# Half sums made one per step, a third wide pair of gate blocks, and a way down that starts later and runs behind every column tile, in a four-layer fp32 trunk on one Trainium2 core

## The chip, the cores and the metric

The kernel runs on 1 core of one Trainium2 chip. The metric is the device time of one execution in microseconds. The kernel before takes 1391.58 us (median of three runs, 1390.59 to 1392.77). The profile quoted below is of one further execution.

## The reference, cut to what matters

A trunk of two layers for 512 tokens of width 1024, all in float32. Each layer is a token mixer (attention in layer 0, a gated linear recurrence in layer 1) and then a gated feed-forward with a short causal convolution. Each of the four parts is normed before and after and added to the residual stream. The feed-forward is the part that most of the change is in:

```python
def conv_ffn(x, w_up, conv_w, conv_b, w_down):          # x 512x1024, w_up 1024x6144, w_down 3072x1024
    u = causal_dwconv(x @ w_up, conv_w, conv_b)          # three taps
    g, v = u[..., :D_FF], u[..., D_FF:]                  # gate and value, 3072 columns each
    return (jax.nn.gelu(g, approximate=True) * v) @ w_down
```

The attention's projection is `x @ w_qkv`, 1024 by 9216.

## The kernel before, in words

**Numbers in two parts.** Every float32 matrix product is made of three matmuls: each operand is split into a high part (written as fp32r by ACT, line 253 for weights) and the rest (by DVE, line 265), and `PASSES` multiplies high by high, high by low and low by high. A unit of weights is one such pair of tiles, `whi` and `wlo`. Eight units exist (`W_UNITS`). After each piece of work on PE the kernel calls `tick()`, which lets side work run (`run_sides`) and calls `pump`, which splits one or two further units in the order of a plan. So a unit is split up to eight units ahead of its use, and ACT and DVE take their work strictly in the order in which it was written.

**Where weights come from.** A plain piece of weights is loaded by SP (line 340) into one of two `raw` buffers of 1 MB; the next load into a buffer stands in SP's queue until both units in it have been split. A piece that is the sum of two pieces of the matrix is built in the one tile `sum`: a first DMA writes one addend (line 309, on SP in the later parts of the kernel), and a second DMA on POOL adds the other (line 311, accumulating). A sum that needs both is a chain: the tile's last reader, the first DMA, the accumulating DMA, then the split on ACT and DVE.

**The feed-forward's way up.** There are 24 gate column blocks and 24 value column blocks of 128, taken in six pairs of steps (`PAIRS`). A plain column tile (`feat_tiles`, `feat`, matmuls on line 436) is 24 matmuls of 128 columns by 512 tokens into a PSUM tile `ps`. In a pair marked True ("wide") the four gate blocks are made together by `sevenths`: seven products of half size in place of eight, each 24 matmuls of 128 columns by 256 tokens (line 870) into `W`, `X` or `Z`, with weights that are sums of weight pieces and right-hand sides `T` that are sums of token halves. The four value blocks of such a pair stay plain tiles. So a plain pair has eight plain tiles; a wide pair has four plain tiles and seven products.

**The token sums.** `token_sums.make` forms the `T`s once per feed-forward, in four names (3, 2, 4, 1), each in two halves `h`: one to three additions on DVE (line 630, tile `run`), a cast on ACT (line 610) at the start of the next step, and the low part on DVE (line 587 or 585) behind the next half's additions. A side task steps through it: one half, then as many ticks as `TOKEN_PACE` says. The attention uses the same helper with a pace of 1.

**The way down.** 3072 rows of `w_down` are done in two units of 1024 rows by seven products each (`down_unit`, `product`, 24 matmuls of 128x512 on line 650, banks `W`, `X`, `vq`) and then 1024 plain rows (`rows_proj`, tiles `acc`). The two units' fourteen products are laid between the column tiles of the later pairs: from step `DOWN_FROM` on, the column tiles are counted f = 0, 1, 2, ..., and a product follows the tiles listed in `DOWN_AT`. I call the products P1 to P14; P1 to P7 are the first unit. The weights of P1, P3, P5 (and P8, P10, P12) are plain pieces (`value`); those of P2, P4, P6, P7 and P9, P11, P13, P14 are in the `sum` tile. P4 and P6 (P11 and P13) only add to what stands in the tile, on POOL alone; P2, P7, P9 and P14 need the first DMA and the accumulating one. The left operands of the products (`A`) are made from the gated columns in `operands`: sums on DVE (line 940), the cast on ACT (944 or 947), the low part on DVE (587, 585 or 953). Results are copied by ACT (line 591, tile `c`), combined on DVE (line 665) and, for the first unit, written to HBM (`down`, line 978, SP).

Of the kernel before, what the change touches and what calls it, by code (L numbers as in the profile page):

```python
# [40 lines left out]
CP_PAD = 8  # L41
WARM = 6

PAIRS = [([0, 1], False), ([2, 3], True), ([4, 5], True), ([6, 7], False), ([8, 9], False), ([10, 11], False)]
DOWN_FROM = 6
DOWN_UNITS = 2
DOWN_AT = (3, 5, 6, 7, 8, 9, 12, 13, 15, 16, 17, 18, 19, 22)
WIDE_STEPS = (1, 3, 1, 2)
TOKEN_PACE = (1, 1, 1, 1, 2, 2, 2, 1)

SHORT_ORDER = [
    ([0, 1], [0, 1, 2]), ([0], [3]), ([2, 3], [0]), ([1], [3]), ([2, 3], [1]), ([2], [2, 3]), ([3], [2, 3]),
# [43 lines left out]
def kernel(  # L96
# [41 lines left out]
    def nm(s):  # L138
        uid[0] += 1
        return f"{s}{uid[0]}"  # L140

    def gen(dt=F32, s="g"):
        return gp.tile([P, 512], dt, tag="g", name=nm(s))
# [45 lines left out]
    raws, units, late, since = {}, {}, [], {}  # L189
# [177 lines left out]
    def side(steps, delay=1, late=False, first=False):  # L367
        sides.insert(0 if first else len(sides), [delay, steps, late])

    def tick():  # L370
        state["tick"] += 1
        run_sides(False)
        if not state["hold"]:
            pump(1 if state["live"] >= W_UNITS - 2 else 2)
        if state["rows"]:
            low_parts()
            loads()
        run_sides(True)
# [201 lines left out]
    def corner(hT, i, j):  # L580
        return lambda a: hT[a][:, 4 * i : 4 * i + 4, j * 256 : (j + 1) * 256]

    def low(lo, whole, hi, flip=False):
        if flip:
            nc.vector.scalar_tensor_tensor(lo, whole, -1.0, hi.bitcast(F32), op0=ALU.mult, op1=ALU.subtract)
        else:
            nc.vector.tensor_tensor(lo, whole, hi.bitcast(F32), op=ALU.subtract)
# [6 lines left out]
    def token_sums(hT):  # L594

        made = {}
        terms_of = {
            3: [((1, 1), 1), ((0, 1), -1)],
            2: [((0, 0), 1)],
            4: [((1, 0), -1)],  # L600
            1: [((0, 0), 1), ((0, 1), -1)],
        }

        def make(pace):
            pace = iter(pace)
            prior, begun = None, []

            def high():
                for hi, lo, a, flip in begun:
                    nc.scalar.activation(hi, a, AF.Copy, scale=-1.0 if flip else 1.0)  # L610

            def lows():
                for hi, lo, a, flip in begun:
                    low(lo, a, hi, flip)
                begun.clear()

            for name in (3, 2, 4, 1):
                hi, lo = (htp.tile([P, 4, 256], F32R, tag="x", name=nm("T"), bufs=8) for _ in range(2))
                made[name] = hi, lo
                parts = [(corner(hT, *ij)(x).bitcast(F32), sg) for ij, sg in terms_of[name] for x in range(2)]  # L620
                if name in (3, 1):
                    first = parts.pop(0)[0]
                    prior = [first[:, 2 * h : 2 * h + 2] for h in range(2)]
                r = [gen(s="run").rearrange("p (k c) -> p k c", k=2) for _ in range(2)]
                for h in range(2):
                    k = slice(2 * h, 2 * h + 2)
                    a = prior[h]
                    high()
                    for b, sg in parts:
                        nc.vector.tensor_tensor(r[h], a, b[:, k], op=ALU.add if sg > 0 else ALU.subtract)  # L630
                        a = r[h]
                    lows()
                    begun.append((hi[:, k], lo[:, k], a, name == 2))
                    yield next(pace)
                prior = r
            high()
            lows()

        return (lambda name: lambda a: made[name][a]), make
# [194 lines left out]
    def ffn(layer, hT, post, pre, spill):  # L834
# [25 lines left out]
        total_of, make = token_sums(hT)  # L860
# [120 lines left out]
        def down_units():  # L981

            ops = (op for n in range(DOWN_UNITS) for op in operands(8 * n))
            for _ in range(2):
                begin_operand(ops)
                end_operand()
                yield
            for n in range(DOWN_UNITS):
                yield from down_unit(n, ops)
            write()  # L990
# [72 lines left out]
        units, at_feat = down_units(), [0]  # L1063
        for js, wide in PAIRS:
            n = state["next"]
            steps = sevenths(js[0], n) if wide else None
            at = iter(WIDE_STEPS if wide else ())

            def between():
                for _ in range(next(at, 0)):  # L1070
                    next(steps, None)
                    tick()
                if j >= DOWN_FROM:
                    f = at_feat[0]
                    if f < 2 or f in DOWN_AT:
                        next(units)
                    if f in DOWN_AT:
                        if f == DOWN_AT[-2]:
                            state["slots"] += 2
                        tick()  # L1080
                    at_feat[0] += 1

            for j in js:
                if j == 11:
                    prep(5)
                if j == 1:
                    side(make(TOKEN_PACE))

                def sink(b, ps):
                    gated(2 if wide else b, ps, 2 * j + b % 2)  # L1090

                feat_tiles(1 if wide else 2, hT, sink, j == 0, between, (n + 3 + 3 * (j - js[0])) if wide else None)
            if wide:
                state["next"] += 9
# [6 lines left out]
    def attention(hT, post, pre, spill):  # L1101
# [411 lines left out]
        total_of, make = token_sums(hT)  # L1513
# [9 lines left out]
        def to_local(p, s, tiles):  # L1523
            local_v[p].extend(tiles)
# [12 lines left out]
        for hp in range(4):  # L1537
            q, k = [], []
            if hp == 0:
                c, o = first_values()  # L1540
                to_local(0, 0, o)
                steps = value_all(c)
                side(make([1] * 8), late=True)
                side(build, late=True)
            v = local_v[hp // 2]
            sink = qk_sink(q, k, False, True, not hp)
            for j in range(2):
                feat_tiles(1, hT, lambda m, ps: sink(2 * j + m, ps), not (hp or j), paired=False)
                step("l", hp, j)
            for hh in range(2):  # L1550
                side(local(2 * hp + hh, hh, q, k, v), 1 + hh)
# [211 lines left out]
    for layer in range(2):  # L1763
# [10 lines left out]
        downs, feats = down_quarters(layer, ends), 0  # L1774
        for js, wide in PAIRS:
            if not wide:
                for j in js:
                    for c0 in (0, D_FF):
                        n = w_cols(w_up, c0 + j * 256, own=False)
                        for m in range(2):  # L1780
                            split_next(n, m)
                            if j >= DOWN_FROM:
                                if feats in DOWN_AT:
                                    next(downs)
                                feats += 1
                continue
            a, b = (j * 256 for j in js)
# [96 lines left out]
```

## Time and profile before

| What | Number |
|---|---|
| Three runs | 1392.77, 1391.58, 1390.59 us; median 1391.58 |
| The profiled execution | 1388.06 us |
| Its span | 1386.3 us |
| Granted TensorE clock, mean | 0.994 |
| PE busy | 98% of the span |
| DVE busy | 74% |
| ACT busy | 50% |

The span is the time from the first instruction to the last in the profiled execution; the execution's own time is 1.8 us more, and the median of the three runs is 3.5 us above the profiled execution. PE matmuls overlap, and the durations that the profile gives them are longer than the distance from one start to the next; I read the cost of a matmul from starts. In the rows, the idle time of an engine before an instruction, and what ended it, stand in brackets. The first feed-forward (layer 0) is the one with times from about 520 to 860 us, the second from about 1040 to 1386 us.

### The profile page before, as it was taken

Reading aid. Unit: us, or ns where it says so; the run is one execution under the profiler, and the core shown is the slowest. Engines: PE = TensorE matmul, PEld = TensorE weight load, DVE = VectorE, ACT = ScalarE, POOL = GpSimd, SP = SyncE. Lnnn points to the kernel's source line nnn. Section 1 sums busy time; section 2 is a strip of 40 time slices with the busy share of each in tenths; the row PEclk is TensorE's granted clock in tenths of the full one; section 3 lists DMA queues with packets and bytes.
Section 4 is the critical chain, followed back from the end, with each engine's and each line's share of the span. In section 5 each row is a group of like instructions: output and inputs, shape, how many; then the busy total and the mean of one; then the engine's idle time right before and its main releaser. Section 6 shows DMA issues by size and latency. Waiting matters only on the chain.

```text
span 1386.3 us, 18707 instructions
## 1 busy us (share of the span) xinstructions
PE 1356.7 (98%) x7109; PEld 1201.8 (87%) x7109; DVE 1027.0 (74%) x1790; ACT 692.7 (50%) x1169; POOL 111.7 (8%) x126
## 2 busy tenths in 40 slices
PE   8989999999999999999999999999999999999997
PEld 6878888888888889898888889888899898888886
DVE  7777574636767689777958769878979777968765
ACT  5434442414355554455645545579664455645542
POOL 2111012011000001000000110000001000000110
PEclk9999999999999999999999999999999999999999
DMA  8878879596648355555668793233154555768671
GB/s 258 226 206 231 227 190 260 192 211 193 224 153 304 100 176 122 149 168 122 199 171 196 209 259 122 92 122 122 62 162 113 152 162 130 208 180 196 197 187 61
DMA packets 184236, 243.10 MB, mean 175 GB/s; under 512 B 16632, under 2 KB 135936, under 8 KB 184146
## 3 DMA queue, kind: packets, MB, share of 16 engines
q1 hardware_dynamic: 151456, 184.82, 40.5%
q0 software_dynamic: 32688, 57.09, 21.4%
q8 instruction: 56, 0.92, 0.3%
q14 instruction: 34, 0.28, 0.1%
q10 hardware_dynamic: 2, 0.00, 0.0%
HBM read 218.23 MB, written 28.36 MB: 178 GB/s over the span
## 4 chain that ended last, share of the span: by engine, by line
PE 47%; DVE 17%; ACT 5%; issue 2%; DMA 1%; DVEq 0%; ACTq 0%; SPq 0%
PE ps L436 24%; PE acc L436 8%; PE X L650 4%; DVE wlo L265 4%; PE vq L650 3%; PE W L650 3%; DVE u L843 2%; PE X L870 2%; DVE run L630 2%; DVE xb L1603 1%; PE Z L870 1%; DVE x L551 1%; PE W L870 1%; ACT whi L253 1%; DMA sum<-in_ffn_w_up_dram 1%
## 5 line engine op out<-in xcount | busy, mean ns | idle before, releaser
L436 PE MATMUL ps<-hT,whi 128*128 128x512 f32 (+1 forms) x2528 | 698.3, 362 | 0.8 <-DVE hT L499 0.6
L436 PEld LDWEIGHTS ps<-hT,whi 128*128 128x128 f32 x2528 | 459.5, 190 | 57.8 <-issue 1.3
L436 PE MATMUL ps<-hT,wlo 128*128 128x512 f32 (+1 forms) x1264 | 456.6, 361 | 4.7 <-DVE wlo L265 4.7
L265 DVE TENSOR_TENSOR wlo<-raw,whi 128x1024 fp32r<-128x1024 f32 x233 | 279.8, 1217 | 36.6 <-ACT whi L253 36.5
L253 ACT ACTIVATE whi<-raw 128x1024 fp32r<-128x1024 f32 x233 | 239.4, 1051 | 120.2 <-DMA raw<-in_attn_w_qkv_dram 87.1
L436 PEld LDWEIGHTS ps<-hT,wlo 128*128 128x128 f32 x1264 | 240.0, 190 | 33.5 <-DVE wlo L265 5.5
L843 DVE SCALAR_TENSOR_TENSOR u<-ps,cols,u 128x511 f32<-128x511 f32 (+1 forms) x160 | 119.6, 747 | 72.0 <-ACT u L839 69.0
L253 ACT ACTIVATE whi<-sum 128x1024 fp32r<-128x1024 f32 x68 | 70.8, 1053 | 124.0 <-DMA sum<-in_attn_w_qkv_dram 70.8
L265 DVE TENSOR_TENSOR wlo<-sum,whi 128x1024 fp32r<-128x1024 f32 x68 | 82.0, 1217 | 43.1 <-ACT whi L253 43.1
L436 PE MATMUL acc<-whi,ahi 128*128 128x512 f32 x256 | 98.2, 383 | 0.0
L436 PE MATMUL acc<-wlo,ahi 128*128 128x512 f32 x256 | 97.1, 379 | 0.3 <-DVE wlo L265 0.3
L436 PE MATMUL acc<-whi,alo 128*128 128x512 f32 x256 | 97.1, 379 | 0.0
L839 ACT ACTIVATE u<-ps,cols 128x512 f32<-128x512 f32 x80 | 61.6, 771 | 39.4 <-PE ps L436 39.2
L853 ACT ACTIVATE u<-u 128x512 f32<-128x512 f32 x48 | 30.3, 631 | 96.5 <-DVE u L843 96.4
L650 PE MATMUL vq<-whi,T 128*128 128x512 f32 x192 | 59.7, 382 | 0.0
L650 PE MATMUL X<-whi,A 128*128 128x512 f32 x192 | 59.0, 379 | 0.0
L436 PEld LDWEIGHTS acc<-whi,alo 128*128 128x128 f32 x256 | 48.4, 189 | 7.3 <-DVE alo L185 0.4
L436 PEld LDWEIGHTS acc<-wlo,ahi 128*128 128x128 f32 x256 | 48.4, 189 | 7.1 <-DVE wlo L265 0.7
L436 PEld LDWEIGHTS acc<-whi,ahi 128*128 128x128 f32 x256 | 48.4, 189 | 6.6 <-ACT ahi L184 0.2
L311 POOL DMA_DIRECT2D sum<-in_ffn_w_down_dram x16 | 20.6, 1289 | 363.4 <-DMA sum<-in_ffn_w_down_dram 124.0
L855 DVE TENSOR_TENSOR u<-u,u 128x512 f32<-128x512 f32 x48 | 33.2, 692 | 13.5 <-ACT u L853 12.4
L650 PEld LDWEIGHTS X<-whi,A 128*128 128x128 f32 x192 | 36.3, 189 | 5.2
(252 smaller groups left out, 1974.9 us busy)
## 6 DMA issues: line engine op xcount, KB each, us to landing
raw<-in_ffn_w_up_dram SPq DMA_DIRECT2D x44, 1024.0 KB
raw<-in_attn_w_qkv_dram SPq DMA_DIRECT2D x25, 1024.0 KB
raw<-in_ffn_w_down_dram SPq DMA_DIRECT2D x16, 1024.0 KB
sum<-in_ffn_w_down_dram POOLq DMA_DIRECT2D x16, 1024.0 KB, 8.8
sum<-in_attn_w_qkv_dram POOLq DMA_DIRECT2D x24, 512.0 KB, 7.8
raw<-in_attn_w_qkv_dram SPq DMA_DIRECT2D x16, 512.0 KB
sum<-in_ffn_w_down_dram SPq DMA_DIRECT2D x8, 1024.0 KB
raw<-in_lru_w_in_dram SPq DMA_DIRECT2D x8, 1024.0 KB
```

The lines of the kernel that those rows point to most:

```text
L253: nc.scalar.activation(hi, raw, AF.Copy)
L265: nc.vector.tensor_tensor(lo, raw, hi.bitcast(F32), op=ALU.subtract)
L311: nc.gpsimd.dma_start(dst, src, accum_op=ALU.add)
L436: mm(dst, l[a], r[b], start=start and n == 0, stop=stop and n == 2)
L551: nc.vector.scalar_tensor_tensor(xh[i], u[i], y, xh[i], op0=ALU.mult, op1=ALU.add)
L630: nc.vector.tensor_tensor(r[h], a, b[:, k], op=ALU.add if sg > 0 else ALU.subtract)
L650: mm(banks[u], act(a)[:, 2 * j + k, u * P : (u + 1) * P], woven(W[b][:, k, :]), start=first and (j, k, n) == (0, 0, 0), stop=(j, k, n) == ...
L839: nc.scalar.activation(u, ps, AF.Identity, scale=cc[:, j : j + 1], bias=cc[:, 48 + j : 49 + j])
L843: nc.vector.scalar_tensor_tensor(u[:, d:], ps[:, : S - d], wc, u[:, d:], op0=ALU.mult, op1=ALU.add)
L853: nc.scalar.activation(u, u, AF.Gelu_apprx_tanh)
L855: nc.vector.tensor_tensor(gv[k], gv[k], u, op=ALU.mult)
L870: mm(bank[:, n * 256 : (n + 1) * 256], W[a][:, k, n * P : (n + 1) * P], woven(act(b)[:, k, :]), start=first and (n, k, p) == (0, 0, 0), st ...
```

## The change

Five edits:

1. The fourth pair (steps 6 and 7) becomes wide: its four gate blocks go through `sevenths`.
2. The way down starts two steps later (`DOWN_FROM` 8 and not 6), so its column tiles are counted over 16 tiles, f = 0 to 15.
3. `DOWN_AT` puts one product behind every column tile from f = 2 to f = 15. Before, the fourteen products stood over f = 3 to 22, with one or two tiles without a product at places: two ahead of P7, one ahead of P9, two ahead of P14.
4. `TOKEN_PACE` is 1 throughout, so the halves of the token sums follow each other at every tick.
5. `make` takes a second argument. In the feed-forward (`behind` true) the cast stands as before at the start of the next step. In the attention (`behind` false) the cast on ACT is written at once behind the half's additions.

```diff
-PAIRS = [([0, 1], False), ([2, 3], True), ([4, 5], True), ([6, 7], False), ([8, 9], False), ([10, 11], False)]
-DOWN_FROM = 6
+PAIRS = [([0, 1], False), ([2, 3], True), ([4, 5], True), ([6, 7], True), ([8, 9], False), ([10, 11], False)]
+DOWN_FROM = 8
 DOWN_UNITS = 2
-DOWN_AT = (3, 5, 6, 7, 8, 9, 12, 13, 15, 16, 17, 18, 19, 22)
+DOWN_AT = (2, 3, 4, 5, 6, 7, 8, 9, 10, 11, 12, 13, 14, 15)
 WIDE_STEPS = (1, 3, 1, 2)
-TOKEN_PACE = (1, 1, 1, 1, 2, 2, 2, 1)
+TOKEN_PACE = (1, 1, 1, 1, 1, 1, 1, 1)
...
-        def make(pace):
+        def make(pace, behind):
             pace = iter(pace)
-            prior, begun = None, []
+            prior, whole, begun = None, [], []
 
             def high():
-                for hi, lo, a, flip in begun:
+                for hi, lo, a, flip in whole:
                     nc.scalar.activation(hi, a, AF.Copy, scale=-1.0 if flip else 1.0)
+                begun.extend(whole)
+                whole.clear()
...
                     lows()
-                    begun.append((hi[:, k], lo[:, k], a, name == 2))
+                    whole.append((hi[:, k], lo[:, k], a, name == 2))
+                    if not behind:
+                        high()
                     yield next(pace)
...
-                    side(make(TOKEN_PACE))
+                    side(make(TOKEN_PACE, True))
...
-                side(make([1] * 8), late=True)
+                side(make([1] * 8, False), late=True)
```

Lines of the changed kernel behind the edits stand two to four lower (630 becomes 632, 650 becomes 654, 870 becomes 874).

The program of the changed kernel shows what moved at three places. The first is ACT in the attention, at the second and third token sums. `T` is a token sum's high part, `run` its additions, `whi` a weight's high part, and `sum` and `raw` the weights' sources; first the kernel before.

```order
L253 ACTIVATE whi105_493<-raw86_374 128x1024
L610 ACTIVATE T94_412<-run97_415 128x512
L1177 ACTIVATE qk111_529<-ps88_377 128x512
L253 ACTIVATE whi112_531<-sum55_231 128x1024
L610 ACTIVATE T107_497<-run109_499 128x512
L253 ACTIVATE whi122_581<-sum55_231 128x1024
L610 ACTIVATE T107_497<-run110_500 128x512
```

The same place in the changed kernel:

```order
L253 ACTIVATE whi105_494<-raw86_374 128x1024
L610 ACTIVATE T107_498<-run109_500 128x512
L1181 ACTIVATE qk111_530<-ps88_377 128x512
L253 ACTIVATE whi112_532<-sum55_231 128x1024
L610 ACTIVATE T107_498<-run110_501 128x512
L253 ACTIVATE whi122_582<-sum55_231 128x1024
```

The cast of `T107`'s first half stood behind the split of a `sum` and now stands ahead of it; every later cast moved up by a step in the same way. DVE's order in the attention is the same in both.

The second place is DVE in the first feed-forward, at the last token sum (name 1: `run992`, `run993` and `T991` before; `run982`, `run983` and `T981` after). `T968` is the sum ahead of it, `w` an output of a wide pair. The kernel before:

```order
L587 TENSOR_TENSOR T968_4975<-run970_4977,T967_4974 128x512
L265 TENSOR_TENSOR wlo985_5084<-sum920_4603,whi984_5083 128x1024
L265 TENSOR_TENSOR wlo995_5128<-raw982_5055,whi994_5127 128x1024
L219 TENSOR_TENSOR sum920_4603<-sum920_4603 128x1024
L843 SCALAR_TENSOR_TENSOR u1000_5188<-ps999_5163,cols364_1815,u1000_5188 128x511
L843 SCALAR_TENSOR_TENSOR u1000_5188<-ps999_5163,cols364_1815,u1000_5188 128x510
L630 TENSOR_TENSOR run993_5121<-hT0780_3932,hT1781_3933 128x512
L630 TENSOR_TENSOR run993_5121<-run993_5121,hT0780_3932 128x512
L630 TENSOR_TENSOR run993_5121<-run993_5121,hT1781_3933 128x512
L587 TENSOR_TENSOR T991_5119<-run992_5120,T990_5118 128x512
L265 TENSOR_TENSOR wlo998_5161<-sum920_4603,whi997_5160 128x1024
```

The changed kernel, from the same low part of `T968`:

```order
L587 TENSOR_TENSOR T968_4975<-run970_4977,T967_4974 128x512
L265 TENSOR_TENSOR wlo977_5019<-raw947_4817,whi976_5018 128x1024
L632 TENSOR_TENSOR run983_5054<-hT0780_3932,hT1781_3933 128x512
L632 TENSOR_TENSOR run983_5054<-run983_5054,hT0780_3932 128x512
L632 TENSOR_TENSOR run983_5054<-run983_5054,hT1781_3933 128x512
L587 TENSOR_TENSOR T981_5052<-run982_5053,T980_5051 128x512
L265 TENSOR_TENSOR wlo985_5061<-raw960_4900,whi984_5060 128x1024
L893 TENSOR_TENSOR w992_5128<-c987_5090,Z991_5103 128x256
L893 TENSOR_TENSOR w993_5129<-c987_5090,Z991_5103 128x256
L587 TENSOR_TENSOR T981_5052<-run983_5054,T980_5051 128x512
L265 TENSOR_TENSOR wlo989_5098<-sum920_4603,whi988_5097 128x1024
```

The last token sum is complete ahead of the split that reads `sum920`, and ahead of the addition on line 219; before, it came behind both.

The third place is SP's queue in the first feed-forward's way down, from the results of P4 on. `down` is a write of results, `raw` a load of plain weights, and `sum` the first DMA of a sum. The kernel before:

```order
L978 DMA down909_4495<-c1101_5939 128x512
L309 DMA sum1062_5659<-in_ffn_w_down_dram 128x4x512
L340 DMA raw1159_6314<-in_ffn_w_down_dram 128x4x512
L978 DMA down909_4495<-c1145_6224 128x512
L978 DMA down909_4495<-c1146_6226 128x512
L340 DMA raw1177_6405<-in_ffn_w_up_dram 128x8x256
L309 DMA sum1062_5659<-in_ffn_w_down_dram 128x4x512
L340 DMA raw1186_6477<-in_ffn_w_up_dram 128x8x256
```

The changed kernel:

```order
L982 DMA down909_4495<-c1144_6288 128x512
L309 DMA sum1102_5983<-in_ffn_w_down_dram 128x4x512
L340 DMA raw1205_6673<-in_ffn_w_up_dram 128x8x256
L309 DMA sum1102_5983<-in_ffn_w_down_dram 128x4x512
L982 DMA down909_4495<-c1185_6545 128x512
L982 DMA down909_4495<-c1186_6547 128x512
L340 DMA raw1217_6728<-in_ffn_w_down_dram 128x4x512
```

The first DMA for P7 (the upper `sum` row) is followed in both by loads, and the first DMA for P9 (the lower one) stands right behind a load of way-up weights, `raw1177` before and `raw1205` after. There are fewer loads between the two, and on PE there is now one column tile between neighbouring products everywhere.

## The prediction

> **What bounds the kernel now.** I read the page's first part and the chain, then the groups of PE's instructions by shape for PE's waits, then the timeline at those waits, and last the timelines of SP, POOL and ACT in the way down. The page first: engine, busy time, share.
>
> ```profile
> span 1386.3 us, 18707 instructions
> PE 1356.7 (98%) x7109; PEld 1201.8 (87%) x7109; DVE 1027.0 (74%) x1790; ACT 692.7 (50%) x1169; POOL 111.7 (8%) x126
> L436 PE MATMUL ps<-hT,wlo 128*128 128x512 f32 x1040 | 395.0, 380 | 4.7 <-DVE wlo L265 4.7
> L870 PE MATMUL X<-T,whi 128*128 128x256 f32 x128 | 25.9, 301 | 6.3 <-DVE T L587 6.3
> L265 DVE TENSOR_TENSOR wlo<-raw,whi 128x1024 fp32r<-128x1024 f32 x233 | 279.8, 1217 | 36.6 <-ACT whi L253 36.5
> ```
>
> PE is the bound: nearly all time is its matmuls, and the two groups of it shown, which wait most, lost 4.7 and 6.3 us. (The last row is for the price of a low part on DVE, 1.22 us.) So a change pays by fewer matmuls or by these waits, and costs wherever it makes PE wait.
>
> **Part 1: the wide pair, fewer matmuls.** PE's timeline gives the price of a product of each shape (start, modelled duration, line, output<-operands).
>
> ```profile
> 575.72 0.39 PE L870 MATMUL Z<-hT,whi 128*128 128x256 f32 x2
> ...
> 578.40 0.60 PE L436 MATMUL ps<-hT,whi 128*128 128x512 f32 x2
> ...
> 685.23 0.38 PE L650 MATMUL W<-whi,A 128*128 128x512 f32 x1
> ...
> 695.59 0.38 PE L650 MATMUL vq<-whi,A 128*128 128x512 f32 x1
> ...
> 716.30 0.38 PE L650 MATMUL X<-whi,A 128*128 128x512 f32 x1
> ```
>
> From 575.72 to 578.40 stand 24 half-size matmuls: 2.68 us. From 685.23 (P5) to 695.59 (P6) stand a product and a column tile, 48 large ones: 10.36 us, 5.18 each. A third wide pair replaces four plain tiles (20.72 us) by seven half-size products (18.76): -1.96 us per feed-forward, **-3.9 us** for both. Its extra copies and additions on ACT and DVE lie beside PE: the second wide pair, the row of 39.48 us below, has DVE busy for 29.20 of it, so I take nothing for them.
>
> **Part 2: the token sums.** The wait is at the last token sum.
>
> ```profile
> 567.86 0.27 PE L870 MATMUL X<-T,whi 128*128 128x256 f32 x1
> ...
> 569.89 0.38 PE L870 MATMUL X<-T,whi 128*128 128x256 f32 x1 [1.76 <-DVE T L587]
> ...
> 572.28 0.58 PE L870 MATMUL X<-T,whi 128*128 128x256 f32 x1 [1.46 <-DVE T L587]
> ```
> ```profile
> 564.51 1.23 DVE L219 TENSOR_TENSOR sum<-sum 128x1024 f32<-128x1024 f32 x1 [2.17 <-DMA sum<-in_ffn_w_up_dram]
> ```
> ```profile
> 93.80:97.00 3.20, 3.19 (x8) 2.56 (x9) 3.20 (x6) 0.00 (x0) 1.97 (x4) 0.54 0.65 95
> 572.60:575.20 2.60, 2.60 (x13) 2.60 (x13) 2.56 (x4) 0.00 (x0) 0.00 (x0) 0.50 0.17 48
> 664.50:695.60 31.10, 31.10 (x146) 27.23 (x145) 29.16 (x41) 18.81 (x26) 2.57 (x2) 1.00 0.71 206
> 578.40:617.88 39.48, 39.48 (x266) 36.91 (x265) 29.20 (x39) 20.88 (x28) 2.60 (x2) 1.00 0.51 136
> ```
>
> The last rows are stretches: length, busy time of PE, weight load, DVE, ACT, POOL, then the granted clock. The product starts at 567.86 and the next at 575.72: 7.86 us where 2.68 is the price. That is 5.18 lost: the two waits, and after them matmuls at a granted clock of 0.50. The second feed-forward shows the same in the group's 6.3 us, so 10.4 for both. After the change the sum's last half is made ahead of the addition on line 219, before which DVE stood idle for 2.17 us, and so more than 6 us before PE wants it: **-10.4 us**. It is less if what is pushed back on DVE becomes late instead; the low end is half.
>
> **Part 3: casts at once in the attention.** PE's longest wait, and DVE and ACT some 40 us ahead of it.
>
> ```profile
> 89.17 0.59 PE L436 MATMUL ps<-hT,whi 128*128 128x512 f32 x2
> ...
> 93.81 0.59 PE L436 MATMUL ps<-hT,wlo 128*128 128x512 f32 x1 [4.04 <-DVE wlo L265]
> ...
> 100.35 0.82 PE L1329 MATMUL S<-qk,qk 128*128 128x128 f32 x4
> ```
> ```profile
> 55.73 0.69 DVE L585 SCALAR_TENSOR_TENSOR T<-run,T 128x512 fp32r<-128x512 f32 x1 [7.99 <-ACT T L610]
> ...
> 57.46 1.20 DVE L265 TENSOR_TENSOR wlo<-sum,whi 128x1024 fp32r<-128x1024 f32 x1
> ...
> 88.48 0.69 DVE L587 TENSOR_TENSOR T<-run,T 128x512 fp32r<-128x512 f32 x1 [2.31 <-ACT T L610]
> ```
> ```profile
> 54.12 1.06 ACT L253 ACTIVATE whi<-sum 128x1024 fp32r<-128x1024 f32 x1 [11.53 <-DMA sum<-in_attn_w_qkv_dram]
> 55.08 0.61 ACT L610 ACTIVATE T<-run 128x512 fp32r<-128x512 f32 x1
> ```
>
> The tile takes 100.35 - 89.17 = 11.18 us where 5.18 is the price: 6.0 lost, 4.0 waiting and the rest at a clock of 0.54. DVE is late there because it stood twice behind a cast that stood on ACT behind something else, at 55.08 behind a split that waited for its DMA. With the cast ahead of that split, DVE does the small work between 55.73 and 57.46, 1.7 us, inside its 7.99, and the 2.31 go: 4.0 us earlier, just what PE waits. **-5.7 us**, between 0 and -6.0. What the casts now hold up on ACT are splits behind them, for the DVE additions of one half; ACT idled 11.5 us there.
>
> Gains together: -3.9 - 10.4 - 5.7 = **-20.0 us**, between -11 and -20.
>
> On the clock there is a rule. The Trainium skill, "TensorE: Matmul & The Clock Gate", section on the HAM clock gate, says that an idle window of about 3.4 us halves PE's clock until it has been busy for about as long. The rows agree in size (0.54 and 0.50), though here two waits of 1.76 and 1.46 were enough. It speaks against this change: a wait that it makes costs more than its length.
>
> **Part 4: the dense way down, where the cost lies.** The first product comes two tiles behind the stage's start; later a product follows each tile, so two products are 20.72 us apart where P5 to P7 had 31.07 (685.23 to 716.30). The chains of first DMA, accumulating DMA and split must fit into that. SP, POOL and ACT (idle before, releaser):
>
> ```profile
> 610.59 0.37 SPq L340 DMA_DIRECT2D raw<-in_ffn_w_down_dram  x1
> ...
> 616.75 1.01 SPq L309 DMA_DIRECT2D sum<-in_ffn_w_down_dram  x1
> ...
> 686.40 0.38 SPq L309 DMA_DIRECT2D sum<-in_ffn_w_down_dram  x1
> ...
> 715.62 0.38 SPq L340 DMA_DIRECT2D raw<-in_ffn_w_up_dram  x1
> 716.05 0.58 SPq L309 DMA_DIRECT2D sum<-in_ffn_w_down_dram  x1
> ...
> 772.59 0.37 SPq L309 DMA_DIRECT2D sum<-in_ffn_w_down_dram  x1
> ```
> ```profile
> 636.44 1.06 ACT L253 ACTIVATE whi<-sum 128x1024 fp32r<-128x1024 f32 x1 [1.25 <-DMA sum<-in_ffn_w_down_dram]
> ...
> 706.24 1.06 ACT L253 ACTIVATE whi<-sum 128x1024 fp32r<-128x1024 f32 x1 [13.71 <-DMA sum<-in_ffn_w_down_dram]
> ...
> 733.00 2.01 ACT L253 ACTIVATE whi<-sum 128x1024 fp32r<-128x1024 f32 x2 [4.29 <-DMA sum<-in_ffn_w_down_dram]
> ...
> 787.44 1.07 ACT L253 ACTIVATE whi<-sum 128x1024 fp32r<-128x1024 f32 x1 [6.37 <-DMA sum<-in_ffn_w_down_dram]
> ```
> ```profile
> 1207.48 0.38 SPq L309 DMA_DIRECT2D sum<-in_ffn_w_down_dram  x1
> ...
> 1234.41 0.58 SPq L309 DMA_DIRECT2D sum<-in_ffn_w_down_dram  x1
> ```
> ```profile
> 1207.27 0.38 PE L650 MATMUL W<-whi,A 128*128 128x512 f32 x1
> ```
> ```profile
> 1224.59 1.06 ACT L253 ACTIVATE whi<-sum 128x1024 fp32r<-128x1024 f32 x1 [10.26 <-DMA sum<-in_ffn_w_down_dram]
> ```
>
> From the first DMA's issue to the split it took 19.7, 19.8, 16.95 and 14.85 us in the first feed-forward, and 17.1 at the second's P7. Each such wait stands in ACT's order, and all behind it waits: the converted columns, the operands of the next product, the splits that free `raw`.
>
> *P7.* Its first DMA goes when the sixth sum's low part is done, 1.2 us behind P5's start (686.40 against 685.23). Behind its landing come a split and a cast on ACT and two low parts on DVE, about 4.5 us (1.06 and 1.22 each). So P5 + 1.2 + 19.8 + 4.5 = 25.5 us where PE wants it at 20.7: 4.8 late; with the second feed-forward's issue at P5 + 0.2 (1207.48 against 1207.27) and its 17.1, 1.1. I take 2.9 as a mean (0 to 5).
>
> *P9.* The new bound. Its first DMA stands in SP's queue behind a load of way-up weights, and that waits until ACT and DVE, released by the seventh sum at 706.24, have split the units that hold its buffer: issue at 716.05, 9.8 us later (second feed-forward: 1224.59 to 1234.41, 9.8). Counting the shorter row of work that the new order puts there, 9.3. Then 16.95 for the two DMAs, then 5.8 of splits, copies, additions and the operand: 32.05 behind the seventh sum, where P7 starts at 4.5. So P9 can follow P7 by 27.5 us; PE wants 20.7. **6.8 late**, in each feed-forward; with the 14.85 of the last chain 4.7, with 19.8 it is 9.7. Before, P9 stood two tiles and a product more behind and this was hidden.
>
> *P2.* Its first DMA now directly follows the load at 610.59, so it is issued some 6 us sooner, about 6.8 before the stage starts; with 19.7 it lands 12.9 into it, and the operand of P1, behind that split on ACT, is ready near 18, where PE wants 15.5: 2.5 late (0 to 4).
>
> *P14.* Issue 0.7 before P12 as now, 14.85 and 4.5: in time; 0.5 for a slower one (0 to 3).
>
> *Clock.* A wait over 4 us was followed by 1.8 us of slow matmuls (6.0 lost less 4.2), so 1.8 for P9's.
>
> Per feed-forward 2.9 + 6.8 + 2.5 + 0.5 + 1.8 = 14.5; both **+29 us** (14 to 38). The sums that only accumulate (P4, P6, P11, P13) have two steps, 20.7 us, for one DMA, and I take nothing. Nor for the plain rows behind the way down, which have no chain of two DMAs.
>
> **Sum.** +29 - 20.0 = +9. Against the profiled execution, 1388.1 + 9 = 1397; its time lies 3.5 us below the median of the runs, so the median goes from 1391.6 to about **1400.6**. What a measurement can tell from no change is 0.2%, 2.8 us.
>
> **The rivals.**
> *The chains fit (faster).* Place: from the first DMA's issue to the split. If it is 14.85 us everywhere, as at 772.59, P2, P7 and P14 are in time and P9 waits 4.7 with 1.8 of slow clock: +13 - 20 = -7, 1385. It decides at about 17 us with all gains kept. For it: one row. Against it: four of five rows are at 17 to 20. Chance 0.21. Were it under 10 us, no wait would be left and the gains alone count: 1372, chance 0.04. The Trainium skill, "DMA: Bandwidth & Descriptors", section on the anatomy of one DMA on the gpsimd path, gives 2.0 us plus the bytes at 436 GB/s, an estimate of 4.4 us for each of these 1 MB transfers; the trace's chains of two took 14.85 and more, so it does not agree.
>
> *Both at their ends (no change).* Waits of 10 in each feed-forward, or gains of 11 beside short waits: 1391.6. Chance 0.10.
>
> *DVE becomes the bound (slower still).* In the densest stretch DVE was busy for 29.16 of 31.10 us. Fourteen such steps in a row leave 0.65 us a step to catch up with what a late sum held back (13.7 us of idle ACT ahead of the seventh), so the products behind P7 and P9 would be late too, by about 5 us a feed-forward: 1411. Against it: the same rows show PE busy for all of that stretch. Chance 0.15.
>
> *The casts or sums change nothing* because another operand is late at the same place: inside my low gains, +6 to +9, within the range.
>
> **How the numbers follow.** Forecast 0.50 (1395 to 1407 by itself); chains fit 0.25 in both forms; no change 0.10; DVE 0.15. Faster by over 0.2%: 0.25; within: 0.11; slower: 0.64. The range, 1383 to 1412, takes in the rivals at 1385 and 1411.
>
> **What would show it.** Right: in the changed profile the waits of X<-T and of 93.81 are gone or under 1 us; PE waits in the way down before P9 for 5 to 9 us on a DVE low part that follows `whi<-sum`, with a smaller wait before P7 and P1; the granted clock dips behind the larger. Wrong: no PE wait over 2 us in the way down (the chains fit), or waits at products that use plain weights (DVE).

## The result, and the profile after

| Kernel | Median, us | Against before |
|---|---|---|
| before | 1392.03 (1390.59 to 1392.77) | |
| changed | 1452.04 (1450.84 to 1453.94) | ratio 1.0434, 95% interval 1.0416 to 1.0452 |

The change makes the kernel 4.3% slower, 60 us; the prediction said 9 us, with a range that ended at 1412. The span of the two profiled executions went from 1386.3 to 1452.2 us, 65.9 more; they lie on different sides of their medians (1388.06 against 1392.03, and 1453.94 against 1452.04).

The changed kernel's page, the lines that answer to those quoted of before, and of its fourth part the chain of waits:

```profile
span 1452.2 us, 19068 instructions
PE 1371.6 (94%) x7253; PEld 1210.4 (83%) x7253; DVE 1040.9 (72%) x1814; ACT 701.9 (48%) x1185; POOL 119.2 (8%) x132
PE 29%; DVE 19%; DMA 12%; ACT 9%; issue 4%; SPq 0%; DVEq 0%; ACTq 0%; POOLq 0%
PE ps L436 14%; DMA sum<-in_ffn_w_down_dram 8%; PE acc L436 7%; DVE wlo L265 5%; DMA raw<-in_ffn_w_up_dram 4%; DVE u L847 3%; PE X L874 2%; ACT whi L253 2%; PE W L874 2%; PE Z L874 1%; PE X L654 1%; DVE xb L1607 1%; ACT u L843 1%; DVE A L944 1%; ACT A L948 1%
```

PE's share fell from 98% to 94%. In the chain, transfers of sums and of way-up weights have come in with 8% and 4%; PE is down to 29%, from 47% before. What PE waited for, from the view of its waits (total, times, longest):

```profile
PE X L654 <- ACT A L948: 25.4, 4, 9.3
PE ps L436 <- DVE wlo L265: 12.5, 5, 5.4
PE W L654 <- DVE wlo L265: 9.6, 2, 4.8
PE X L654 <- DVE wlo L265: 7.9, 6, 1.9
PE W L654 <- ACT A L948: 4.3, 3, 2.2
```

These are nearly all in the two ways down: `X` and `W` on line 654 are its products, and four of the five `ps` waits are column tiles there. The waits that parts 2 and 3 of the prediction were about are gone. The groups by shape, and the attention's tile on PE:

```profile
L874 PE MATMUL X<-T,whi 128*128 128x256 f32 x192 | 32.8, 275 | 0.0
```
```profile
89.50 0.38 PE L436 MATMUL ps<-hT,whi 128*128 128x512 f32 x1
...
94.68 0.60 PE L1333 MATMUL S<-qk,qk 128*128 128x128 f32 x3
```

X<-T waits for nothing, and the tile takes 5.18 us where it took 11.18. So both gains are there in full. The loss is in the way down. Its products at which PE waited, in the first feed-forward, between the stage's first tile and its end:

```profile
647.63 0.60 PE L436 MATMUL ps<-hT,whi 128*128 128x512 f32 x2
...
706.50 0.38 PE L654 MATMUL W<-whi,A 128*128 128x512 f32 x1
...
731.25 0.48 PE L654 MATMUL X<-whi,A 128*128 128x512 f32 x1 [3.86 <-ACT A L948]
733.64 0.79 PE L654 MATMUL X<-wlo,A 128*128 128x512 f32 x1 [1.91 <-DVE wlo L265]
...
758.37 0.48 PE L654 MATMUL W<-whi,A 128*128 128x512 f32 x1 [1.58 <-ACT A L948]
763.65 0.79 PE L654 MATMUL W<-wlo,A 128*128 128x512 f32 x1 [4.80 <-DVE wlo L265]
...
798.26 0.38 PE L654 MATMUL W<-whi,A 128*128 128x512 f32 x1
...
808.48 0.80 PE L436 MATMUL ps<-hT,wlo 128*128 128x512 f32 x1 [4.44 <-DVE wlo L265]
...
833.78 0.80 PE L654 MATMUL X<-whi,A 128*128 128x512 f32 x1 [7.43 <-ACT A L948]
836.18 0.79 PE L654 MATMUL X<-wlo,A 128*128 128x512 f32 x1 [1.60 <-DVE wlo L265]
...
843.55 0.38 PE L436 MATMUL acc<-whi,ahi 128*128 128x512 f32 x1
```

706.50 is P5, 731.25 P7, 758.37 P9, 798.26 P12, 808.48 the tile ahead of P13, 833.78 P14. The stage takes 843.55 - 647.63 = 195.9 us. It holds 16 column tiles and 14 products, 30 times 5.18 = 155.4 us of PE, so 40.5 are lost; the second feed-forward loses 44.2 (from 1203.39 to 1402.95, in the same view). In the kernel before, the same stage up to P14's end, with seven tiles more, took 191.7 us and lost nothing:

```profile
617.88 0.38 PE L436 MATMUL ps<-hT,whi 128*128 128x512 f32 x1
...
809.54 0.38 PE L436 MATMUL ps<-hT,whi 128*128 128x512 f32 x1
```

So the stage did not get shorter when tiles were taken out of it. Something other than PE sets its length. The ledger of the span: -3.9 fewer matmuls, -10.4 token sums, -6.0 attention, +84.7 ways down, +1.5 elsewhere, which is +65.9.

The chains of sums in the changed kernel, on SP, POOL and ACT:

```profile
713.41 0.38 SPq L309 DMA_DIRECT2D sum<-in_ffn_w_down_dram  x1
...
738.09 0.38 SPq L340 DMA_DIRECT2D raw<-in_ffn_w_up_dram  x1
738.53 0.57 SPq L309 DMA_DIRECT2D sum<-in_ffn_w_down_dram  x1
...
792.47 0.38 SPq L340 DMA_DIRECT2D raw<-in_ffn_w_up_dram  x1
...
813.39 0.37 SPq L309 DMA_DIRECT2D sum<-in_ffn_w_down_dram  x1
```
```profile
671.77 1.28 POOL L311 DMA_DIRECT2D sum<-in_ffn_w_down_dram  x1 [22.16 <-DVE wlo L265]
697.73 1.30 POOL L311 DMA_DIRECT2D sum<-in_ffn_w_down_dram  x1 [24.68 <-DVE wlo L265]
```
```profile
684.10 1.05 ACT L253 ACTIVATE whi<-sum 128x1024 fp32r<-128x1024 f32 x1
...
694.24 1.04 ACT L253 ACTIVATE whi<-sum 128x1024 fp32r<-128x1024 f32 x1
...
729.19 1.06 ACT L253 ACTIVATE whi<-sum 128x1024 fp32r<-128x1024 f32 x1 [15.45 <-DMA sum<-in_ffn_w_down_dram]
...
756.31 1.06 ACT L253 ACTIVATE whi<-sum 128x1024 fp32r<-128x1024 f32 x1 [8.88 <-DMA sum<-in_ffn_w_down_dram]
...
801.14 1.06 ACT L253 ACTIVATE whi<-raw 128x1024 fp32r<-128x1024 f32 x1 [5.35 <-DMA raw<-in_ffn_w_up_dram]
...
831.73 1.06 ACT L253 ACTIVATE whi<-sum 128x1024 fp32r<-128x1024 f32 x1 [15.45 <-DMA sum<-in_ffn_w_down_dram]
```

The first DMA for P7 is issued at 713.41, 6.9 us behind P5's start, where it had been 1.2; the one for P14 at 813.39, 15.1 behind P12, where it had been 0.7 ahead. The accumulating DMAs on POOL wait on the low part of the sum before (`wlo`). From P4's (671.77) to P6's (697.73) are 26.0 us: 12.3 until ACT splits the sum's first unit at 684.10, and 13.6 more until the second unit, split only at 694.24, has its low part and frees the tile. So about half of this link is the order of the splits and not the transfer. And ahead of P13 there is a wait on a plain load that the kernel before didn't have: `raw` is asked for at 792.47, split at 801.14, and the tile at 808.48 waits for it.

### The profile page after: what moved, and what is told of

Its sections match the earlier page's. It is cut to its first block, busy times and chain, and to the rows that moved or that the text cites. A ratio compares the mean times of both kernels' runs of the same rounds, so it can differ in the third digit from the quotient of the medians.

```text
span 1452.2 us, 19068 instructions
## 1 busy us (share of the span) xinstructions
PE 1371.6 (94%) x7253; PEld 1210.4 (83%) x7253; DVE 1040.9 (72%) x1814; ACT 701.9 (48%) x1185; POOL 119.2 (8%) x132
## 4 chain that ended last, share of the span: by engine, by line
PE 29%; DVE 19%; DMA 12%; ACT 9%; issue 4%; SPq 0%; DVEq 0%; ACTq 0%; POOLq 0%
PE ps L436 14%; DMA sum<-in_ffn_w_down_dram 8%; PE acc L436 7%; DVE wlo L265 5%; DMA raw<-in_ffn_w_up_dram 4%; DVE u L847 3%; PE X L874 2%; ACT whi L253 2%; PE W L874 2%; PE Z L874 1%; PE X L654 1%; DVE xb L1607 1%; ACT u L843 1%; DVE A L944 1%; ACT A L948 1%
## 5 line engine op out<-in xcount | busy, mean ns | idle before, releaser
L436 PE MATMUL ps<-hT,whi 128*128 128x512 f32 (+1 forms) x2400 | 661.9, 362 | 0.8 <-DVE hT L499 0.6
L436 PEld LDWEIGHTS ps<-hT,whi 128*128 128x128 f32 x2400 | 436.1, 190 | 54.3 <-ACT whi L253 1.3
L436 PE MATMUL ps<-hT,wlo 128*128 128x512 f32 (+1 forms) x1200 | 433.9, 362 | 12.5 <-DVE wlo L265 12.5
L436 PEld LDWEIGHTS ps<-hT,wlo 128*128 128x128 f32 x1200 | 228.5, 190 | 40.9 <-DVE wlo L265 14.5
L253 ACT ACTIVATE whi<-sum 128x1024 fp32r<-128x1024 f32 x74 | 77.2, 1049 | 160.8 <-DMA sum<-in_ffn_w_down_dram 88.1
L847 DVE SCALAR_TENSOR_TENSOR u<-ps,cols,u 128x511 f32<-128x511 f32 (+1 forms) x144 | 107.6, 747 | 53.5 <-ACT u L843 50.9
L265 DVE TENSOR_TENSOR wlo<-sum,whi 128x1024 fp32r<-128x1024 f32 x74 | 89.3, 1219 | 48.8 <-ACT whi L253 48.8
L654 PE MATMUL X<-whi,A 128*128 128x512 f32 x192 | 66.6, 421 | 25.7 <-ACT A L948 25.4
L843 ACT ACTIVATE u<-ps,cols 128x512 f32<-128x512 f32 x72 | 55.2, 766 | 15.1 <-PE ps L436 15.1
L654 PE MATMUL vq<-whi,T 128*128 128x512 f32 x192 | 59.7, 382 | 0.0
L587 DVE TENSOR_TENSOR A<-A,A 128x1024 fp32r<-128x1024 f32 x12 | 14.7, 1224 | 57.0 <-ACT A L948 57.0
```

What stands on the lines that cost most here:

```text
L253: nc.scalar.activation(hi, raw, AF.Copy)
L265: nc.vector.tensor_tensor(lo, raw, hi.bitcast(F32), op=ALU.subtract)
L436: mm(dst, l[a], r[b], start=start and n == 0, stop=stop and n == 2)
L654: mm(banks[u], act(a)[:, 2 * j + k, u * P : (u + 1) * P], woven(W[b][:, k, :]), start=first and (j, k, n) == (0, 0, 0), stop=(j, k, n) == ...
L843: nc.scalar.activation(u, ps, AF.Identity, scale=cc[:, j : j + 1], bias=cc[:, 48 + j : 49 + j])
L847: nc.vector.scalar_tensor_tensor(u[:, d:], ps[:, : S - d], wc, u[:, d:], op0=ALU.mult, op1=ALU.add)
```

## The experiments

After the result I held this theory: **eight sums go one after the other through one tile, each waiting for the splits of the last, and these splits stand in one order with the splits of plain loads; this loop has a length of its own, about 195 us, that the tiles taken out had covered.** (That the loop has a fixed length did not hold, as the kernel without the third wide pair shows.) Rivals: the third wide pair spoils the start of the stage; ACT and DVE have too much to do with a product behind every tile; `pump` asks for the splits too late. A time without a range is that of one run; eleven runs of the kernel before, made beside some of these, went from 1386.38 to 1393.97 us, so the times of single runs that lie less than some 8 us apart decide nothing, and the traces have to.

**The gains alone.** The changed kernel with the pairs and the way down of before.

```diff
-PAIRS = [..., ([6, 7], True), ...]
-DOWN_FROM = 8
-DOWN_AT = (2, 3, 4, 5, 6, 7, 8, 9, 10, 11, 12, 13, 14, 15)
+PAIRS = [..., ([6, 7], False), ...]
+DOWN_FROM = 6
+DOWN_AT = (3, 5, 6, 7, 8, 9, 12, 13, 15, 16, 17, 18, 19, 22)
```

> Only the half sums at every step and the casts at once; pairs and way down as in the kernel before. If the ledger of the changed kernel holds, the waits of X<-T (5.2 and 5.2 us) and of the attention (6.0) go and nothing comes back: 1392 - 16 = 1375.5 us. If these two edits also cost something later (casts holding up splits, sums pushing splits back on DVE), 1380 or more.

Measured 1371.45 us (1371.19 to 1371.97), ratio 0.9867, interval 0.9847 to 0.9886. This kernel beats both: PE is busy for 99% of its span, and its ways down take 191.7 us each, as before, with no wait.

```profile
span 1369.5 us, 18713 instructions
PE 1350.9 (99%) x7109; PEld 1198.3 (87%) x7109; DVE 1026.0 (75%) x1790; ACT 692.4 (51%) x1169; POOL 111.7 (8%) x126
```

**Each of the two alone**, with everything else as in the kernel before: `make([1] * 8, False)` and the old pace; or pace 1 throughout and `make([1] * 8, True)`.

> The kernel before with only the casts at once in the attention. The prediction's third part: 6 us faster, 1385. If the casts cost something elsewhere, less.

> The kernel before with only the half sums of the feed-forwards at every step. The prediction's second part: 10.4 us faster, 1380. If pushing the splits back on DVE costs, 5 us or less.

Measured 1383.54 us (ratio 0.9948, interval 0.9931 to 0.9964) and 1378.67 us (0.9909, 0.9891 to 0.9927): -0.5% and -0.9%, that is 7 and 13 us with 2 to 3 us of uncertainty each. Both parts of the prediction hold, and neither costs anything elsewhere that these runs can tell.

**Dense way down without the third wide pair.** The changed kernel with `([6, 7], False)`.

> The changed kernel with its third wide pair turned back into a plain one: the way down still starts at step 8 and is dense. Chain theory (eight sums through one tile need about 195 us, whatever PE has to do beside them): the way down stays as long as in the changed kernel, the plain pair costs 3.9 us more, 1456 us. Rival (the third wide pair keeps the sum tile and the raw buffers busy into the way down, and that is what makes it late): most of the 85 us go, 1400 us or less.

Measured 1431.24 us: neither expectation. Against the kernel with the gains alone, at 1371.45, the dense way down costs 60 us by itself, and the third wide pair on top another 21, where it should save 4. So the rival is right in part, and the theory is not right as it stood: with the same tiles, products and sums the stages take 184.0 and 184.6 us, so the loop has no fixed length of 195 us. Of the 26.9 us that both stages lose more with the third pair (84.7 against 57.8), 17.6 are at P7. Without it the step from P4's accumulating DMA to P6's takes 19.6 us (667.29 to 686.88) and not 26.0, and P7 was in time: its first DMA was issued at 705.24, ahead of P5 at 706.95.

```profile
705.24 0.38 SPq L309 DMA_DIRECT2D sum<-in_ffn_w_down_dram  x1
```
```profile
706.95 0.38 PE L654 MATMUL W<-whi,A 128*128 128x512 f32 x1
```

The waits at P9, at the tile ahead of P13 and at P14 are there as in the changed kernel (its longest 4.8, 4.6 and 7.0 us).

**A short accumulating DMA.** The changed kernel, with this in place of the accumulating DMA's line; it adds 64 of the 512 columns and leaves the rest of the second addend out:

```diff
-                nc.gpsimd.dma_start(dst, src, accum_op=ALU.add)
+                n = 64 if cols == 512 and i >= state["lagging"] else m
+                nc.gpsimd.dma_start(dst[:, :, :n], src[:, :, :n], accum_op=ALU.add)
```

> The changed kernel, but the accumulating DMA of each way-down sum adds 64 of its 512 columns, so most of the second addend is left out. Chain theory: each of the eight links gets about 6 us shorter, which is 48 us of the 40 lost in each way down: the waits go or shrink to under 15 us per feed-forward, 1375 to 1400 us. Rival (DVE and ACT have too much to do per column tile, or the loads of plain weights come too late on their own): less than 15 us gained, 1437 us or more.

Measured 1400.23 us, 52 us less: just past the end of what the chain theory allowed. The median from issue to landing went from 8.9 to 3.6 us. Of 40.5 and 44.2 us lost, 16.5 and 14.6 are left, at P9 and P14 for the most part. The tile ahead of P13 waits no more, though the plain loads still have two buffers: that load was late because the sums were.

**Two units at every tick.** `pump` splits one unit per tick once six are live; here it splits two in the way down (the lines that set `dense` there are left out).

```diff
-            pump(1 if state["live"] >= W_UNITS - 2 else 2)
+            pump(1 if state["live"] >= W_UNITS - 2 and not state["dense"] else 2)
```

> The changed kernel, but in the way down pump may split two units at each tick also when six or more are live, so that the splits can run the full eight units ahead. If the lost look-ahead comes from pump's own brake, sums are split two units (about 7 us of PE) sooner and P7, P9 and P14 win that: 1452 - 30 = 1420 us or less. Chain theory: the splits are late because what they read has not landed, and asking sooner changes little: 1445 to 1455 us.

Measured 1474.37 us: 22 us slower, which neither foresaw. The view of PE's waits shows where, and ACT's timeline the split ahead of P7:

```profile
PE ps L436 <- DVE u L847: 67.1, 6, 20.1
PE W L654 <- ACT A L948: 11.0, 4, 5.6
```
```profile
728.32 1.06 ACT L253 ACTIVATE whi<-sum 128x1024 fp32r<-128x1024 f32 x1 [14.20 <-DMA sum<-in_ffn_w_down_dram]
729.28 0.76 ACT L843 ACTIVATE u<-ps,cols 128x512 f32<-128x512 f32 x1
```

Asked for sooner, the split of a sum stands sooner on ACT, waits there for the same landing, and now has a convolution of a column tile (line 843) behind it. That convolution empties a PSUM tile, so PE waits for a place to write. In this order without overtaking, asking early was no better than asking late.

**A second tile for sums, and first DMAs sent early.** P7's and P14's sums get a tile of their own; there is room for it only with two general tiles and one bias table fewer, so that has a control. In the second kernel the first DMAs may also go ahead of plain loads that stand before them in the plan.

```diff
+        if i in second:
+            total["two"] = total["two"] or cp.tile([P, 1, 4, 512], F32, tag="gain2", name=nm("sum"))
+            tile_ = total["two"]
...
-            if i < state["raw"] and total["open"] and after[i] in finished:
+            if (i < state["raw"] or i in early) and total["open"] and after[i] in finished:
```

> The changed kernel with two general tiles and one bias table fewer, as a control for the next two, which need the room. Both theories: 1452 us, within 5.

> The changed kernel with a second tile for sums: P2, P4, P6 (P9, P11, P13) are summed in one, P7 (P14) in the other, so that the first DMA of P7, P9 and P14 need not wait for the low part of the sum just ahead. Chain theory: the waits around P7 (9 us) and P14 (12) in each feed-forward go for the most part, P9's load order stays as it is: 1452 - 40 = 1412 us. Rival (the splits are late because plain loads, ACT or DVE are late): less than 15 us gained.

> As the kernel with a second sum tile, and the first DMAs of P2, P7, P9 and P14 may go ahead of the plain loads that stand before them in the plan. Chain theory: P9's 8 us in each feed-forward go too, and what is left is the wait of a column tile behind a late load (7 us each): 1390 to 1400 us. Rival: as for the second tile alone, 1437 us or more.

Measured 1457.17 for the control, 1423.34 for the second tile and 1399.22 us for both (ratio to before 1.0073, interval 1.0052 to 1.0094). So -34 and another -24, where the theory said -40 and then 1390 to 1400 us. In the last kernel no product waits for its sum for as much as 1 us; of the 12.1 and 11.6 us that its ways down still lose, most is at single column tiles (2.4 of the 11.3 below lie in the attention):

```profile
PE ps L440 <- DVE wlo L266: 11.3, 5, 5.4
...
PE ps L440 <- DVE u L851: 2.5, 1, 2.5
```

**First DMAs on POOL.** `nc.gpsimd` in place of `nc.sync` on line 309.

> The changed kernel with every first DMA issued by POOL and not by SP. If P9 is late because its first DMA stands behind a load in SP's queue, as the prediction had it, it goes 3 us sooner in each feed-forward: 1446 us. If what counts is the seventh sum's own low part, nothing changes: 1452, within 3.

Measured 1450.39 us, one run, 1.6 less than the changed kernel: by its time alone inconclusive. In the trace P9 starts in time and its loss falls from 9.6 to 6.1 and 3.8 us, as the prediction had it for a first DMA that stands behind a load; but its second half still waits, the waits at the neighbours stay, and of the 12 us that the ways down gain in all (36.5 and 35.8 are lost), 8.7 are lost again between the two.

**A third buffer for plain loads**, in the control with fewer buffers (`RAW_BUFS = 3`).

> The control with fewer buffers, and three buffers for plain loads in place of two; one sum tile as in the changed kernel. Chain theory: the waits that end on a plain load (the column tile between P12 and P13, 7 us, and the first DMA of P9 behind its load, some 5) go, and those at P7 and P14 stay: 1457 - 25 = 1432 us. Rival (late plain loads are the cause of all): 1400 us or less. If loads wait on the splits in any case: 1450 or more.

Measured 1413.73 us: 43 us less than the control, more than expected. The tile ahead of P13 no longer waits; around P7 3.6 and 6.0 us are lost in the two feed-forwards and not 9.1 and 9.0, around P9 6.9 and 3.3 and not 10.2 and 9.4, around P14 9.0 and 9.8 and not 12.1 and 12.8. So plain loads and sums are not two causes side by side: a plain load that comes late holds up the next sum's split, and a late sum holds up the split that frees a buffer.

**Both at once.** The third buffer and the short accumulating DMA.

> The kernel with a third buffer for plain loads, and in it the accumulating DMAs of the way down cut to 64 of 512 columns (most of the second addend is left out). If sums and loads together are all that makes PE wait, under 8 us of waits are left in each feed-forward: 1375 to 1395 us. If ACT and DVE have too much to do for one product per column tile: 1400 or more.

Measured 1382.54 us. The ways down take 157.4 and 157.3 us, 2 more than PE's work. The stage in the first feed-forward (length; busy time of PE, weight load, DVE, ACT, POOL; clock):

```profile
670.00:812.00 142.00, 140.30 (x651) 122.54 (x650) 110.65 (x158) 80.20 (x116) 12.07 (x13) 1.00 0.47 140
```

PE is busy for 140.3 of 142 us with a product behind every tile, and DVE for 110.7. So ACT and DVE can carry the dense way down: the rival of the prediction in which DVE becomes the bound falls, and late sums and plain loads are the loss of the two stages but for 2 us in each. (The third buffer alone left 19.5 and 19.1, the short DMA alone 16.5 and 14.6.) The kernel as a whole is still 11 us slower than the one with the gains alone, though it has a wide pair more: beside these 4 us it loses time ahead of the first way down, for the most part in the attention, and the cause of that is not shown.

**What the third wide pair adds.** Two kernels: its gated ends (four convolutions and gates) run at every tick and not at every second (`yield 2 if j < 6 else 1`); and, in the control with fewer buffers, a tile for the way down's sums alone, so that the pair need not hand its own over, with P2's DMAs ahead of the loads.

> The changed kernel, but the third wide pair's four gate blocks are convolved and gated at every tick and not at every second one, so that this work of ACT and DVE is done before the way down's sums need them. If that work is what makes the third pair's way down later than the plain pair's (21 us between the two kernels), P7's waits of 9 us in each feed-forward go: 1430 us. If the third pair's price comes from the one sum tile being handed over late, nothing goes: 1448 to 1455 us.

> The control with fewer buffers, and one tile for the way down's sums alone, so that the third wide pair need not hand its own over; the first DMA and the accumulating one of P2 go ahead of the loads in front of them. The eight sums still share one tile. If the late handover is what the third wide pair costs (21 us more than a plain one there): 1457 - 20 = 1437 us or less, with P7 in time. If not: 1450 or more, the waits as in the control.

Measured 1458.42 and 1458.78 us: no gain. The handover is not the cause: in the second of them P2's first DMA went at 612.75, where it went at 644.26 in the control, and yet P4's accumulating DMA went at 676.21 (676.91) and P7 lost as much as there. What sets P4's time in it is the order of the splits, not the tile. With the ends sooner the wait around P7 shrank from 9 us to about 5.5 and some 5 appeared at P1 and P2, so this work costs wherever it stands in that stretch; whether it is all of the 21 us is not settled.

## Why the prediction was wrong, point by point

**Parts 1 to 3 were right.** The third wide pair's steps from 608.15 to 647.63 take 39.5 us, as the pair of before did; the token sums gave 10.4 (10.4 predicted), the attention 6.0 (5.7). The runs show the last two alone and together.

**Part 4 failed, by +84.7 where it said +29.** Its mechanism was there: late sums, waits on DVE's low parts behind `whi<-sum`, and a lower clock behind them. The size was wrong, at P7 and P14 above all and at one place that was not in the sum. Loss per feed-forward, from starts, waits and slow matmuls together:

| Place | Predicted | Measured, first and second |
|---|---|---|
| P1 and P2 | 2.5 | 1.0 and 2.1 |
| P7 | 2.9 | 8.7 and 8.9 |
| P9 | 6.8 + 1.8 clock | 9.6 and 9.6 |
| tile ahead of P13 | 0 | 7.2 and 7.4 |
| P14 | 0.5 | 12.2 and 14.5 |
| others | 0 | 1.8 and 1.7 |

P9 was worked out from the event that releases it: 9.3 us from the seventh sum's split to its first DMA, which is what the rows show (729.19 to 738.53), then the two DMAs (17.8 us to the split, 16.95 taken). It came out right. P7 and P14 were worked out from the place on PE at which their first DMAs had been issued before: "1.2 us behind P5's start" and "0.7 before P12 as now". That is the step that failed. These places were no property of the order; they were the look-ahead that column tiles without a product had built up. In the dense order the sums ahead (P4, P6, P13) were themselves late, and I had taken nothing for those: "The sums that only accumulate (P4, P6, P11, P13) have two steps, 20.7 us, for one DMA". In place of 20.7 us, the step from P4's accumulating DMA to P6's took 26.0, and that from P11's to P13's 24.2 (765.13 to 789.36). The first DMA for P7 came 6.9 us behind P5's start and the one for P14 15.1 behind P12's, that is 5.7 and 15.8 later than taken. The chains behind them were not the main error: 15.8 us to the split at P7, where I had taken 17 to 20, and 18.3 at P14, where I had 14.85.

The first and the last of the eight accumulating DMAs on POOL in the trace of before:

```profile
626.04 1.28 POOL L311 DMA_DIRECT2D sum<-in_ffn_w_down_dram  x1 [38.84 <-DVE u L843]
...
778.55 1.28 POOL L311 DMA_DIRECT2D sum<-in_ffn_w_down_dram  x1 [20.48 <-DMA sum<-in_ffn_w_down_dram]
```

They are 21.8 us apart on average, in a stage where PE waited for nothing and so set the pace. In the changed kernel they are 24.4 apart (648.33 to 819.09), in an order with seven tiles fewer. The old distance alone would not have told the loss: with the third buffer and the short DMA they are 21.6 apart, and that stage lost 2.0 us. What the loop takes by itself no run isolates. I priced four of the eight links one by one, and did not follow how the lateness of one is handed on to the next.

**The tile ahead of P13** was a class of wait that the prediction left out: a plain load, whose buffer is freed by splits that stand behind a late sum. The run with a third buffer shows that it feeds back on the sums, and the one with the short DMA that it comes from them. Among the prediction's own signs of being wrong were "waits at products that use plain weights"; this is such a wait, at a column tile, but with another cause than the one named there.

**Clock.** I took 1.8 us a feed-forward, for P9 alone. PE's waits in the view above come to 59.7 us, 58 without one in the attention, of the 84.7; the rest are a few short waits and matmuls at a lower clock behind the waits, some 25 us where I had 3.6. The stretches around P9 and P14 (length; busy of PE, weight load, DVE, ACT, POOL; clock):

```profile
758.40:781.80 23.40, 18.60 (x72) 15.64 (x73) 14.36 (x20) 10.84 (x17) 1.29 (x1) 0.85 0.65 179
803.40:843.50 40.10, 26.63 (x97) 21.55 (x97) 23.54 (x34) 19.62 (x29) 5.96 (x7) 0.79 0.55 158
```

**Rivals.** "The chains fit" needed 17 us from first DMA to split; the rows have 15.8 (713.41 to 729.19), 17.8 and 18.3, so the chains by themselves were close to its limit and to what I had taken; it fell because they began late. The estimate from the Trainium skill's page "DMA: Bandwidth & Descriptors" (section on the anatomy of one DMA on the gpsimd path), 4.4 us, stays far from the 8.9 from issue to landing. "DVE becomes the bound" named a price nearer the truth for a cause that the run with both the third buffer and the short DMA rules out.

**The sums of the prediction.** Its low end of the gains, -11, is not the sum of the low ends that it gives for the parts (-3.9, half of 10.4, and 0 make -9.1), and +38 with -11 would have put the upper end at about 1419 and not at 1412. The measured 1452 lies outside either. Of the seven tiles taken out, one stood ahead of P1 and one between P1 and P2, beside the five that the list of the edits names.

## What to carry to other kernels

When a change takes work out of a stage, ask what else has a length there: follow the serial resource (one tile, two buffers) round its whole loop in the new order, each link starting where the one before it ends, and not from where it started in the old order. A margin that an old trace shows at one place belongs to the old order; work it out again from the event that releases it. When a bundle of edits loses, run its parts alone: two of them are worth 1.3% here without the others.

## What the runs showed of the hardware that I had not expected

The clock can fall after two short waits: 1.76 and 1.46 us, 2.4 us apart, were followed by a clock of 0.50 for 2.6 us in the kernel before, and in the changed kernel 1.58 and 4.80 around P9 by one of 0.85 over 23 us. It does not always: in the kernel with the third buffer, 1.16 and 1.91 us, 2.4 us apart, ahead of and in P7 of the first feed-forward were followed by a clock of 1.00. What decides it these runs don't show. An accumulating DMA takes 3.6 us for 128 KB and 8.9 for 1 MB, median from issue to landing, in the same place of the same program.
